# Queries stored raw and rotated one head ahead, one root for all heads, the late modulations moved into the merge stage

## The chip, the cores and the metric

The kernel runs on one core of a Trainium2 chip. The metric is the time of one execution in microseconds on the device. Of the core's engines this text speaks of TensorE (PE in the profile: matrix products, with its weight loads as PEld), VectorE (DVE), ScalarE (ACT), GpSimd (POOL) and SyncE (SP, which issues most of the DMAs). Each engine has a queue of its own, in which its instructions stand in a fixed order.

## What is computed

One layer of a diffusion backbone: 1024 latent tokens of width 1024, a context of 256 tokens, everything in float32. Cut to what matters here:

```python
mod_lat = silu(c) @ w_mod + b_mod                 # 9 pieces ml[0..8]; mc[..] for the context
x  = x  + 0.5*ml[2] * swiglu(modulate(rms_norm(x,  norm1_g), ml[0], ml[1]), ffn1_w_in, ffn1_w_out)
cx = cx + 0.5*mc[2] * swiglu(modulate(rms_norm(cx, norm1_g), mc[0], mc[1]), ffn1_w_in, ffn1_w_out)
hx, hc = modulate(rms_norm(x, norm2_g), ml[3], ml[4]), modulate(rms_norm(cx, norm2_g), mc[3], mc[4])
bg, cg, vc, q, k, v, gates = split(hx @ w_in)     # keys and values of the context from hc
y_conv = bg * short_conv(cg * vc, conv_w)
q, k = rotate(rms_norm(q, q_norm_g)), rotate(rms_norm(k, k_norm_g))   # 8 query heads, 2 key heads of 128
o = attend(q, concat(k_ctx, k), concat(v_ctx, v))
g_conv, g_attn = split(sigmoid(gates))
x  = x + ml[5] * ((g_conv * (y_conv @ w_branch_conv) + g_attn * (o @ w_branch_attn)) @ w_out)
x  = x + 0.5*ml[8] * swiglu(modulate(rms_norm(x, norm3_g), ml[6], ml[7]), ffn2_w_in, ffn2_w_out)
return rms_norm(x, final_g)
```

## The kernel before

**Products.** Every float32 operand of a product is split into a high part (rounded by ACT, a CAST in the profile) and a low part (the difference, taken by DVE or POOL), and each product of 128 columns is three matmuls: high by high, high by low, low by high. The large products against `w_in` and `ffn_w_in` are made by a Winograd scheme: POOL and DVE form sums of weight tiles (`s`), DVE their low parts (`wl`), and DVE and ACT combine the results out of PSUM (tiles `u`, `v`, `b`, `c`).

**Stages.** In the profile the first FFN takes about 140 to 980 us, the products of `w_in` (the "mix" stage, a list of 26 jobs `mix_jobs`) 980 to 1531, attention 1531 to 1945, the merge with `w_branch_attn` 1945 to 2040, `w_out` to 2140, and the second FFN and the end the rest.

**Order.** The body of the kernel is written as Python generators that are stepped against each other (`run(steps, n)` takes n steps). A scheduler then replays the recorded program with a timeline of its own and sets each engine's order by it, within the pools: `apool` (tag "A", 38 buffers of 128x1024), `tpool` (11 of 128x512), `wpool` for weights (3 raw, 4 high and 4 low), and PSUM banks (5 `ps`, 2 `pt`, 1 `po`). All instructions are recorded by one helper (L88), so a row of the profile is told by its tile names. Buffer names carry running numbers, which differ between the two programs.

**Mix (L1360 and on).** A job "uv" multiplies two results to `u`; from the third on it also runs 13 steps of the late modulations (`late_steps`, L1056 and L1368): modulation pieces 6, 7 and 8, each as two halves, each half 8 steps of a 256 KB load `rawm` and one DVE operation on `macc`, then `acch`, `accl` and a small product whose row goes to DRAM and back as `mcol`. What is left of them runs in the second FFN (L1766). Jobs "conv" write `yd`, jobs "gates" write sigmoids to `gad`. Job "k" and the four jobs "q" go through `turned` (L1267): for each result tile the 32-row pieces are swapped by DMA within SBUF into `sw`; ACT squares into `sq`; 8 small matmuls with `ones` sum the squares into PSUM; DVE multiplies by the cosine table, POOL multiplies `sw` by the sine table, DVE adds. For queries the root is left for later: `query_norm` takes the sums, finds the reciprocal root by ten small DVE operations per head and chunk (`rsqrt_cols`, tiles `rs_y` and `rs_t`) and keeps it in `rq`; the rotated query goes to DRAM (`qd`). For keys the root is broadcast and multiplied in before the store to `kd`. `turning_tables` makes the two tables by 16 PE transposes and 4 DVE operations, once for the keys and, at the first "q" job, once for the queries.

**Attention (L1407 on).** `k_ctx`, `keys_values(0)`, `v_ctx`, two weight tiles `wc` and the eight tiles `y` of the first chunk are loaded and split. 16 units (8 heads by 2 chunks of 512 queries) follow. `Unit.begin` loads 256 KB of `qd`, ACT rounds it and POOL takes the low part (`qs`). `scores` multiplies with keys, DVE takes maxima (`m`, `nm`) and multiplies by the query's root, ACT takes the exponential with that root as its scale. Products of the conv branch (`y`, `wc`) fill the gaps.

**Merge.** `merge(j, ch)` is called for 8 column blocks by 2 chunks; 14 of the 16 calls stand in the loop after attention. Each is 24 matmuls, then DVE on `ga` and `z`.

## Time and profile before

| | us |
|---|---|
| median of 3 runs | 2788.38 (2787.86 to 2788.5) |
| the profiled execution | 2791.95 |
| its span | 2790.2 |
| mean granted PE clock | 0.977 |

Engines' busy times, the stretches and the single stalls on which the argument rests stand in the prediction. In a window row the columns are: the stretch, its length, then for PE, PEld, DVE, ACT and POOL the busy time and (x) the instructions, the granted PE clock, the busy share of the DMA engines, and GB/s. A timeline row is: start, length, engine, line, operation, out<-in, shape, count, and in brackets the idle time before it with what ended it. In the list of tiles, three numbers with slashes are the shortest, the median and the longest in ns. Of the DMA issues the columns are the queue, the count, the size of each and the median us from issue to landing.

### The profile page before, as it was taken

Reading aid. Unit: us, or ns where it says so; the run is one execution under the profiler, and the core shown is the slowest. Engines: PE = TensorE matmul, PEld = TensorE weight load, DVE = VectorE, ACT = ScalarE, POOL = GpSimd, SP = SyncE. Lnnn points to the kernel's source line nnn. Section 1 sums busy time; section 2 is a strip of 40 time slices with the busy share of each in tenths; the row PEclk is TensorE's granted clock in tenths of the full one; section 3 lists DMA queues with packets and bytes.
Section 4 is the critical chain, followed back from the end, with each engine's and each line's share of the span. In section 5 each row is a group of like instructions: output and inputs, shape, how many; then the busy total and the mean of one; then the engine's idle time right before and its main releaser. Section 6 shows DMA issues by size and latency. Waiting matters only on the chain. (4 is left out here: it accounts for less than half of the span.)

```text
span 2790.2 us, 36733 instructions
## 1 busy us (share of the span) xinstructions
PE 2680.9 (96%) x13135; PEld 2230.4 (80%) x13135; DVE 2052.5 (74%) x3508; ACT 1149.8 (41%) x2144; POOL 567.9 (20%) x383
## 2 busy tenths in 40 slices
PE   7898999999999989999989999999999999999998
PEld 4687888888878867887868778887888788888888
DVE  5887688877877888768778576677547886567885
ACT  4524333333444632322324566666225333334443
POOL 2240112222010033233332111100000443221200
PEclk8899999999999999999999999999999999999999
DMA  8265433444984345334345421101443552327831
GB/s 302 91 202 156 140 122 99 129 132 156 321 201 109 113 146 179 121 106 129 110 125 158 146 91 59 46 23 35 147 136 106 181 167 91 101 78 268 196 87 61
DMA packets 374176, 374.27 MB, mean 134 GB/s; under 512 B 29782, under 2 KB 257256, under 8 KB 373992
## 3 DMA queue, kind: packets, MB, share of 16 engines
q1 hardware_dynamic: 364968, 354.61, 39.4%
q0 software_dynamic: 9024, 17.30, 3.8%
q8 instruction: 103, 1.69, 0.2%
q14 instruction: 81, 0.66, 0.1%
HBM read 295.77 MB, written 70.78 MB: 131 GB/s over the span
## 5 line engine op out<-in xcount | busy, mean ns | idle before, releaser
L88 PE MATMUL ps<-r,wl 128*128 128x512 f32 x5784 | 1365.7, 395 | 41.9 <-DVE wl L88 15.7
L88 PEld LDWEIGHTS ps<-r,wl 128*128 128x128 f32 x5784 | 1091.8, 190 | 281.3 <-DVE wl L88 21.9
L88 ACT CAST wl<-s 128x512 fp32r<-128x512 f32 x280 | 172.7, 619 | 373.6 <-PE ps L88 291.8
L88 ACT CAST wl<-raw 128x512 fp32r<-128x512 f32 x298 | 184.1, 619 | 300.2 <-PE ps L88 178.9
L88 POOL TENSOR_TENSOR s<-raw 128x512 f32<-128x512 f32 x70 | 104.2, 1489 | 936.5 <-DMA raw<-in_ffn_w_in_dram 531.3
L88 DVE TENSOR_TENSOR wl<-raw,wl 128x512 fp32r<-128x512 f32 x296 | 213.8, 723 | 94.1 <-ACT wl L88 93.0
L88 DVE TENSOR_TENSOR wl<-s,wl 128x512 fp32r<-128x512 f32 x280 | 240.1, 858 | 11.0 <-ACT wl L88 9.4
L88 POOL TENSOR_TENSOR s<-raw,s 128x512 f32<-128x512 f32 x70 | 112.3, 1604 | 447.2 <-DVE wl L88 436.3
L88 DVE SCALAR_TENSOR_TENSOR macc<-rawm,silu_c,macc 128x512 f32<-128x512 f32 x168 | 144.8, 881 | 9.4 <-DMA rawm<-in_w_mod_dram 8.6
L88 DVE TENSOR_REDUCE m<-ps 128x1 f32<-128x512 f32 (+1 forms) x192 | 111.2, 594 | 54.7 <-PE ps L88 53.5
L88 DVE TENSOR_TENSOR u<-u,ps 128x512 f32<-128x512 f32 x186 | 126.3, 680 | 32.4 <-PE ps L88 31.7
L88 DVE TENSOR_TENSOR pts<-pt,pts 128x512 fp32r<-128x512 f32 x160 | 108.5, 684 | 32.7 <-ACT pts L88 31.6
L88 PE MATMUL po<-pts,vl 128*128 128x512 f32 x384 | 130.0, 422 | 1.7 <-ACT pts L88 1.5
L88 PE MATMUL ps<-rh,wl 128*128 128x512 f32 x360 | 123.5, 393 | 2.8 <-ACT rh L88 2.8
L88 ACT CAST rh<-hid 128x512 fp32r<-128x512 f32 x132 | 81.2, 620 | 102.9 <-PE ps L88 85.9
L88 ACT CAST pts<-pt 128x512 fp32r<-128x512 f32 x160 | 91.5, 592 | 74.3 <-PE pt L88 72.4
L88 POOL TENSOR_TENSOR s<-raw,raw 128x512 f32<-128x512 f32 x70 | 107.9, 1541 | 23.0 <-DMA kcd<-kx 8.7
L88 PE MATMUL ps<-kl,qs 128*128 128x512 f32 x384 | 107.4, 399 | 1.2 <-ACT pc L88 1.0
L88 POOL TENSOR_TENSOR s<-s,raw 128x512 f32<-128x512 f32 x70 | 104.4, 1492 | 20.4 <-issue 5.8
L88 DVE TENSOR_TENSOR rl<-hid,rh 128x512 fp32r<-128x512 f32 x132 | 89.7, 684 | 21.8 <-PE ps L88 13.0
L88 PE MATMUL ps<-rh,wh 128*128 128x512 f32 x300 | 102.4, 389 | 0.0
L88 ACT ACTIVATE pl<-ps,nm,rq 128x512 f32<-128x512 f32 x128 | 98.5, 780 | 0.0
(308 smaller groups left out, 4635.7 us busy)
## 6 DMA issues: line engine op xcount, KB each, us to landing
raw<-in_ffn_w_in_dram SPq DMA_DIRECT2D x117, 512.0 KB, 4.6
raw<-in_ffn_w_out_dram SPq DMA_DIRECT2D x72, 512.0 KB, 5.3
rawm<-in_w_mod_dram SPq DMA_DIRECT2D x128, 256.0 KB, 3.6
raw<-in_w_in_dram SPq DMA_DIRECT2D x61, 512.0 KB, 4.6
hid<-hd SPq DMA_DIRECT2D x40, 512.0 KB, 9.3
ws<-in_ffn_w_out_dram POOLq DMA_DIRECT2D x30, 512.0 KB, 6.3
hd<-c SPq DMA_DIRECT2D x38, 256.0 KB, 2.0
hd<-u SPq DMA_DIRECT2D x38, 256.0 KB, 3.9
```

What stands on the lines that cost most here:

```text
L88: inst = getattr(self.engine, name)(*args, **kw)
```

## The change

- **Late modulations.** The uv jobs no longer run them. The merge loop takes one late step at every step of a merge (8 a merge, 112 of the 114 steps in the 14 merges), the loop in the second FFN takes what is left. So 32 operations on `macc` (with 8 MB of loads) leave the mix stage and 16 leave the second FFN; all 48 now stand at the end of attention and in the merge.
- **Queries.** A "q" job squares, sums by the 16 small matmuls, adds the sums to `rq` by one DVE operation for two heads, and stores the raw result. The DMAs into `sw`, 32 DVE operations of 128x512 and 16 POOL operations of 128x512 leave the mix stage, and so do the roots; one `rsqrt_cols` over 64 columns is put behind the last sums.
- **Rotation.** `turning_tables(0)` and `prepare_query(0)` stand at the end of the mix stage, behind the last product. `prepare_query` loads a whole head (512 KB) and, in four pieces, its swapped rows (512 KB), and POOL multiplies both and adds: three operations of 128x1024 a head, 24 in all. Head 1 is prepared at the start of attention, head n/2+1 in the even units n. `begin` splits a slice of the prepared head and loads nothing.
- **Keys.** Both multiplications and the addition are on POOL (12 operations of 128x512 there instead of 4, 8 fewer on DVE), and the roots are taken per head, so four times ten small operations on four columns in place of two times ten on eight.

```diff
@@ -224,10 +224,9 @@
             matmul(ps, wh, xl, start=False, stop=False)
             matmul(ps, wl, xh, start=False, stop=(i == last))
 
-    def rsqrt_cols(a, n):
-
-        y = small("rs_y", n)
-        t = small("rs_t", n)
+    def rsqrt_cols(a, n, yt=None):
+
+        y, t = yt or (small("rs_y", n), small("rs_t", n))
         dve.tensor_scalar(
             out=y[:].bitcast(I32), in0=a.bitcast(I32), scalar1=-0.5, scalar2=1597463007.0,
             op0=ALU.mult, op1=ALU.add,
@@ -1264,7 +1263,27 @@
                        pinned=True)
         return pss
 
-    def turned(dst, h0, ab, ch, tabs, norm):
+    def rsqrt_sums(pss):
+        a = small("rs_a", 4)
+        dve.tensor_scalar(out=a[:], in0=pss, scalar1=HD * EPS, scalar2=None, op0=ALU.add)
+        return rsqrt_cols(a[:], 4)
+
+    def queries(h0, ab, ch):
+
+        sq = atile("sq", (P, 2, 512))
+        for h, t in enumerate(ab):
+            act.activation(out=sq[:, h], in_=t, func=AF.Square)
+            sp.dma_start(out=qd[h0 + h, :, ch[1] : ch[1] + 512], in_=t)
+        yield
+        c0 = ch[1] // P
+        dve.tensor_scalar(
+            out=rq[:].rearrange("p (h t) -> p h t", t=KD)[:, h0 : h0 + 2, c0 : c0 + 4],
+            in0=square_sums([sq[:, h] for h in range(2)]).rearrange("p (h t) -> p h t", t=4),
+            scalar1=HD * EPS, scalar2=None, op0=ALU.add,
+        )
+        yield
+
+    def keys(ab, ch, tabs):
 
         o = ch[1]
         sw, sq = atile("sw", (P, 2, 512)), atile("sq", (P, 2, 512))
@@ -1273,36 +1292,31 @@
                 sp.dma_start(out=sw[a : a + 32, h], in_=t[b : b + 32])
             act.activation(out=sq[:, h], in_=t, func=AF.Square)
         yield
-        scale = norm(square_sums([sq[:, h] for h in range(2)]))
+        pss = square_sums([sq[:, h] for h in range(2)])
         for h, t in enumerate(ab):
-            dve.tensor_mul(out=t, in0=t, in1=tabs[0][:, o : o + 512])
+            pool.tensor_mul(out=t, in0=t, in1=tabs[0][:, o : o + 512])
             pool.tensor_mul(out=sw[:, h], in0=sw[:, h], in1=tabs[1][:, o : o + 512])
-            dve.tensor_add(out=t, in0=t, in1=sw[:, h])
-            if scale is None:
-                sp.dma_start(out=dst[h0 + h, :, o : o + 512], in_=t)
-        yield
-        if scale is not None:
-            for h, t in enumerate(ab):
-                pr = bcast(scale[:, 4 * h : 4 * h + 4], 512)
-                dve.tensor_mul(out=t, in0=t, in1=pr)
-                sp.dma_start(out=dst[h0 + h, :, o : o + 512], in_=t)
-        yield
-
-    def query_norm(h0, ch):
-        def norm(pss):
-            c0 = h0 * KD + ch[1] // P
-            for h in range(2):
-                a = small("ssq", 4)
-                dve.tensor_scalar(out=a[:], in0=pss[:, 4 * h : 4 * h + 4], scalar1=HD * EPS, scalar2=None, op0=ALU.add)
-                y = rsqrt_cols(a[:], 4)
-                dve.tensor_copy(out=rq[:, c0 + h * KD : c0 + h * KD + 4], in_=y[:])
-
-        return norm
-
-    def key_norm(pss):
-        a = small("ssk", 8)
-        dve.tensor_scalar(out=a[:], in0=pss, scalar1=HD * EPS, scalar2=None, op0=ALU.add)
-        return rsqrt_cols(a[:], 8)
+            pool.tensor_add(out=t, in0=t, in1=sw[:, h])
+        scale = [rsqrt_sums(pss[:, 4 * h : 4 * h + 4]) for h in range(2)]
+        yield
+        for h, t in enumerate(ab):
+            pr = bcast(scale[h], 512)
+            dve.tensor_mul(out=t, in0=t, in1=pr)
+            sp.dma_start(out=kd[h, :, o : o + 512], in_=t)
+        yield
+
+    q_turned = {}
+
+    def prepare_query(hd, tabs):
+
+        q, sw = atile("q"), atile("qsw")
+        load(q[:], qd[hd])
+        for a, b in swapped:
+            load(sw[a : a + 32], qd[hd, b : b + 32])
+        pool.tensor_mul(out=q[:], in0=q[:], in1=tabs[0][:])
+        pool.tensor_mul(out=sw[:], in0=sw[:], in1=tabs[1][:])
+        pool.tensor_add(out=q[:], in0=q[:], in1=sw[:])
+        q_turned[hd] = q
 
     def context_keys(pc):
         k, sq = ttile("kx"), ttile("ksq")
@@ -1311,9 +1325,7 @@
         later.append(context_keys_normed(k, sq))
 
     def context_keys_normed(k, sq):
-        a = small("ssk", 4)
-        dve.tensor_scalar(out=a[:], in0=square_sums([sq]), scalar1=HD * EPS, scalar2=None, op0=ALU.add)
-        y = rsqrt_cols(a[:], 4)
+        y = rsqrt_sums(square_sums([sq]))
         yield
         pr = bcast(y, 512)
         dve.tensor_scalar(
@@ -1364,8 +1376,6 @@
             for ch, cg, vc in pairs_of:
                 dve.tensor_mul(out=u[:, ch[1] : ch[1] + 512], in0=cg, in1=vc)
             run(normc2, 3)
-            if i > 1:
-                run(late_steps, 13)
         elif what == "conv":
             u = us.pop(i)
             for ch, bg, gc in pairs_of:
@@ -1389,17 +1399,17 @@
         elif what == "v":
             later.append(latent_values(pairs_of))
         else:
-            if i == 0:
-                tabs = turning_tables(int(what == "k"))
+            if what == "k":
+                tabs = turning_tables(1)
             for ch, a, b in pairs_of:
-                if what == "k":
-                    work = turned(kd, 0, (a, b), ch, tabs, key_norm)
-                else:
-                    work = turned(qd, 2 * i, (a, b), ch, tabs, query_norm(2 * i, ch))
+                work = keys((a, b), ch, tabs) if what == "k" else queries(2 * i, (a, b), ch)
                 next(work)
                 later.append(work)
+    tabs = turning_tables(0)
+    prepare_query(0, tabs)
     while later:
         run_later()
+    rstd_q = rsqrt_cols(rq[:], NQ * KD, [const.tile([P, NQ * KD], F32, name=f"rsq_{i}") for i in range(2)])
 
 
     k_lat, v_lat = {}, {}
@@ -1461,10 +1471,9 @@
             self.hd, self.ch, self.g = hd, ch, hd // (NQ // NKV)
 
         def begin(self):
-            o, q = self.ch[1], ttile("q")
-            load(q, qd[self.hd, :, o : o + 512])
+            o = self.ch[1]
             self.qs = [ttile("qs", dt=F32R) for _ in range(2)]
-            split(q, *self.qs, pool)
+            split(q_turned[self.hd][:, o : o + 512], *self.qs, pool)
             self.pc = atile("pc", (P, 4, CT))
             self.pl = []
             self.rsum = small("rsum", 4)
@@ -1492,10 +1501,10 @@
                 parts.append((pl[:, j * 512 : (j + 1) * 512], ps))
             dve.tensor_reduce(out=nm[:], in_=m3[:], axis=AX.X, op=ALU.max, negate=True)
             c = self.hd * KD + self.ch[1] // P + qt
-            dve.tensor_mul(out=nm[:], in0=nm[:], in1=rq[:, c : c + 1])
+            dve.tensor_mul(out=nm[:], in0=nm[:], in1=rstd_q[:, c : c + 1])
             for j, (dst, ps) in enumerate(parts):
                 act.activation(
-                    out=dst, in_=ps, func=AF.Exp, bias=nm[:], scale=rq[:, c : c + 1], accum_out=rs[:, j : j + 1]
+                    out=dst, in_=ps, func=AF.Exp, bias=nm[:], scale=rstd_q[:, c : c + 1], accum_out=rs[:, j : j + 1]
                 )
             dve.reduce_sum(out=self.rsum[:, qt : qt + 1], in_=rs[:], axis=AX.X)
 
@@ -1579,6 +1588,7 @@
     units = [Unit(hd, ch) for hd in range(NQ) for ch in (C0, C1)]
     u = units[0]
     u.begin()
+    prepare_query(1, tabs)
     run(conv_out(C0, 0))
     conv_weights(2)
     u.scores(0)
@@ -1612,6 +1622,8 @@
         u.begin()
         if n_unit == 4:
             keys_values(1)
+        if n_unit % 2 == 0 and n_unit < 14:
+            prepare_query(n_unit // 2 + 1, tabs)
         for n in (3, 2, 3, 2):
             u.scores(len(u.pl))
             for _ in range(n):
@@ -1636,7 +1648,9 @@
     for j in range(KD):
         for ch in (C0, C1):
             if (j, ch) not in ((0, C0), (1, C0)):
-                run(merge(j, ch))
+                step = merge(j, ch)
+                for _ in step:
+                    run(late_steps, 1)
     xs = Latents("x2")
     gain3 = norm_gain("gain3", 6, "g3")
     fast = Winograd(xs, gain3["l"], modl, 6, column_pairs(ffn2_w_in[0], ffn_offsets), ahead=AH3)
```

How the scheduler places this shows at three places. The first is SP's queue around the last gates of the mix stage (their stores are `gad`). Of before, up to the last of them (`kd`, `vd` hold keys and values, `yd` the conv inputs):

```order
L88 DMA kc_13471<-kcd 128x512
L88 DMA kl_13475<-kd 128x512
L88 DMA kl_13479<-kd 128x512
...
L88 DMA y_13507<-yd 128x512
...
L88 DMA y_13535<-yd 128x512
L88 DMA gad<-c_13348 128x512
L88 DMA raw_13576<-in_w_branch_conv_dram 128x8x128
L88 DMA q_13539<-qd 128x512
L88 DMA gad<-b_13384 128x512
...
L88 DMA gad<-u_13347 128x512
```

And of the change:

```order
L88 DMA gad<-c_12823 128x512
L88 DMA rope_12948<-in_rope_dram 128x512
...
L88 DMA gad<-b_12859 128x512
L88 DMA gad<-v_12858 128x512
L88 DMA gad<-u_12822 128x512
L88 DMA q_12980<-qd 128x1024
L88 DMA qsw_12981<-qd 32x1024 x4
L88 DMA kc_13002<-kcd 128x512
L88 DMA kl_13006<-kd 128x512
L88 DMA kl_13010<-kd 128x512
...
L88 DMA y_13038<-yd 128x512
```

All loads of attention stood ahead of the store of the last gate; now they all stand behind it, with the head's 1 MB first.

The second is PE's queue from the last product of the mix stage on. Of before:

```order
L88 MATMUL ps_13449<-r_1541_8839,wl_13403 128x512 x3
L88 MATMUL ps_13547<-y_13507,wc_13496 128x512 x2
L88 MATMUL ps_13547<-y_13507,wc_13497 128x512
L88 MATMUL ps_13547<-y_13511,wc_13496 128x512 x2
L88 MATMUL ps_13547<-y_13511,wc_13497 128x512
```

And of the change:

```order
L88 MATMUL ps_12924<-r_1541_8839,wl_12878 128x512 x3
L88 MATMUL pt_12949<-ident,rope_12948 128x128 x4
L88 MATMUL pt_12957<-ident,rope_12956 128x128 x4
L88 MATMUL pt_12965<-ident,rope_12964 128x128 x4
L88 MATMUL pt_12973<-ident,rope_12972 128x128 x4
L88 MATMUL ps_13086<-y_13038,wc_13027 128x512
L88 MATMUL ps_13121<-kc_13002,qs_13070 128x256 x2
L88 MATMUL ps_13130<-kl_13006,qs_13070 128x512 x2
L88 MATMUL ps_13135<-kl_13010,qs_13070 128x512 x2
```

Before, 24 matmuls of the conv branch (eight tiles `y`) came ahead of the first scores; now the transposes of the tables come, one conv matmul, and then the scores with the first head's `qs`.

The third is POOL's queue in the change, at the keys (`rope` are the tables, `s` the weight sums of the products that run meanwhile):

```order
L88 TENSOR_TENSOR c_10251<-c_10251,rope_10440 128x512
L88 TENSOR_TENSOR sw_10474<-sw_10474,rope_10441 128x512
L88 TENSOR_TENSOR c_10251<-c_10251,sw_10474 128x512
L88 TENSOR_TENSOR b_10311<-b_10311,rope_10440 128x512
L88 TENSOR_TENSOR sw_10474<-sw_10474,rope_10441 128x512
L88 TENSOR_TENSOR u_10250<-u_10250,rope_10440 128x512
L88 TENSOR_TENSOR sw_10486<-sw_10486,rope_10441 128x512
L88 TENSOR_TENSOR b_10311<-b_10311,sw_10474 128x512
L88 TENSOR_TENSOR s_1878_10720<-raw_10718 128x512
```

Before, only the products with the sine table stood here, and DVE had the others.

## The prediction

> **What bounds the kernel now.** First the head of the page and its chain of waits:
>
> ```profile
> span 2790.2 us, 36733 instructions
> PE 2680.9 (96%) x13135; PEld 2230.4 (80%) x13135; DVE 2052.5 (74%) x3508; ACT 1149.8 (41%) x2144; POOL 567.9 (20%) x383
> PE 40%; DVE 3%; DMA 1%; ACT 1%; issue 1%; POOL 0%; SPq 0%; DVEq 0%; ACTq 0%; POOLq 0%
> ```
>
> PE is busy for 96% of the span, and the chain is PE with short visits to others. Work taken from DVE or POOL is worth something only where PE waits, so I read windows of 20 us:
>
> ```profile
> 1060.00:1080.00 20.00, 20.00 (x90) 16.55 (x89) 13.23 (x20) 6.56 (x11) 10.53 (x7) 1.00 0.60 190
> 1100.00:1120.00 20.00, 17.00 (x64) 13.59 (x65) 15.71 (x26) 6.29 (x12) 8.09 (x6) 0.83 0.41 132
> 1300.00:1320.00 20.00, 15.76 (x67) 12.04 (x65) 20.00 (x55) 2.49 (x4) 6.47 (x4) 0.99 0.61 184
> 1460.00:1480.00 20.00, 15.44 (x73) 13.15 (x74) 17.74 (x31) 4.52 (x8) 8.94 (x6) 0.75 0.28 81
> ```
>
> A full window holds 90 large matmuls at clock 1.00, 0.222 us each. The windows that fall short lie where the late modulations or the query rotation run. The timeline names the stalls, on PE (first four rows) and on DVE:
>
> ```profile
> 1103.00 3.35 PE L88 MATMUL ps<-r,wl 128*128 128x512 f32 x7 [4.47 <-ACT wl L88]
> 1321.54 3.78 PE L88 MATMUL ps<-r,wl 128*128 128x512 f32 x8 [5.52 <-ACT u L88]
> 1434.25 5.30 PE L88 MATMUL ps<-r,wl 128*128 128x512 f32 x22 [3.22 <-DVE wl L88]
> 1464.56 5.73 PE L88 MATMUL ps<-r,wl 128*128 128x512 f32 x13 [8.50 <-DVE wl L88]
> 1092.07 6.60 DVE L88 SCALAR_TENSOR_TENSOR macc<-rawm,silu_c,macc 128x512 f32<-128x512 f32 x7 [0.90 <-DMA rawm<-in_w_mod_dram]
> 1428.91 0.69 DVE L88 TENSOR_TENSOR c<-c,rope 128x512 f32<-128x512 f32 x1 [4.90 <-DMA sw<-c]
> 1456.31 0.69 DVE L88 TENSOR_TENSOR c<-c,rope 128x512 f32<-128x512 f32 x1 [3.99 <-DMA sw<-c]
> 1456.92 1.29 DVE L88 SCALAR_TENSOR_TENSOR rs_y<-rs_t,rs_y 128x4 f32<-128x4 f32 x2
> 1462.48 0.23 DVE L88 SCALAR_TENSOR_TENSOR rs_t<-rs_y 128x4 f32<-128x4 f32 x2
> 1458.09 1.26 POOL L88 TENSOR_TENSOR s<-raw 128x512 f32<-128x512 f32 x1
> ```
>
> Seven `macc` hold DVE for 6.60 us and PE waits 4.47; twice DVE waits for the swapped rows, and behind it the small root operations take 1.29 us for what takes 0.23 when POOL is idle.
>
> **Mix stage: -29.** The idle times add up to 4.47 + 5.52 + 3.22 + 8.50 = 21.7 us. The first matmuls after them are slow: 7, 8, 22 and 13 took 18.16 us where 50 x 0.222 = 11.1 would do, so 7.1 more. All of it comes from operations that leave the stage: 28.8, taken as -29. The bounds are the idle time alone, -22, and -33 if smaller stalls of the same windows go too. What remains of a query job (squares, the small matmuls, one addition) is off the path.
>
> What would pay in the second FFN is nothing: PE fills this window with the `macc` in it.
>
> ```profile
> 2200.00:2320.00 120.00, 120.00 (x531) 99.13 (x530) 96.87 (x130) 37.60 (x63) 50.37 (x35) 1.00 0.53 163
> ```
>
> **The start of attention: +17.** Call the end of the last product T.
>
> ```profile
> 1530.69 0.61 PE L88 MATMUL ps<-y,wc 128*128 128x512 f32 x2
> 1532.28 5.28 PE L88 MATMUL ps<-y,wc 128*128 128x512 f32 x22 [0.97 <-DVE wc L88]
> 1519.74 4.33 SPq L88 DMA_DIRECT2D y<-yd  x6
> y<-yd SPq DMA_DIRECT2D x8, 256.0 KB, 6.0
> gcd<-b SPq DMA_DIRECT2D x1, 256.0 KB, 2.0
> 1534.85 0.64 ACT L88 ACTIVATE u<-u 128x512 f32<-128x512 f32 x1 [0.67 <-DVE u L88]
> 1532.07 0.62 ACT L88 CAST qs<-q 128x512 fp32r<-128x512 f32 x1 [0.32 <-DMA q<-qd]
> L88 POOL TENSOR_TENSOR wc<-raw,wc 128x1024 fp32r<-128x1024 f32 x9 | 21.6, 2395 | 111.5 <-ACT wc L88 111.5
> 1185.55 1.03 PE L88 MATMUL pt<-ident,rope 128*128 128x128 f32 x8
> 1528.61 1.89 DVE L88 TENSOR_TENSOR y<-y 128x512 fp32r<-128x512 f32 x3
> 1430.79 1.74 DVE L88 TENSOR_TENSOR c<-c,sw 128x512 f32<-128x512 f32 x1 [0.59 <-POOL sw L88]
> ```
>
> At T = 1530.69 PE went straight on, since the `y` loads had been issued by 1524. In the change they stand behind the last gate's store. That store waits for a DVE sum (0.67) and a sigmoid (0.64) after the last product: about T+1.5. SP then issues the head and its four swapped pieces at 4.33/6 = 0.72 each, to T+5.1; with 2.0 us of landing the head is there at T+7. POOL's three operations of 128x1024 take 3 x 2.395 = 7.2, ACT's rounding 0.62: the first scores can run at T+14.9. The first `y` is the thirteenth issue (five, then seven loads, then itself), at T+10, ready near T+13; only one matmul runs on it before the scores. PE has 16 transposes, 2 us, until then: 12.9 idle. To that come 2.8 us of slow matmuls (13 after the 8.50 stall took 5.73 for 2.9), and about 3 for DVE, which now takes 14 low parts here (0.63 alone, by the row of three; 1.74 beside POOL). What the start costs today, 2, goes: 12.9 + 2.8 + 3 - 2 = 17. Bounds: 9, if issues take 0.38 as single ones do and the low parts keep pace, and 26, if POOL's operations stretch by a third and half the low parts take 1.74.
>
> **Keys: +5.** POOL now has a train of 12 rotations with 4 `s` between, and the DVE rows ahead of the next `wl` hold some 38 small operations.
>
> ```profile
> 1200.00:1220.00 20.00, 18.70 (x90) 15.19 (x89) 12.32 (x45) 1.28 (x3) 4.60 (x4) 0.91 0.13 46
> 1190.72 1.82 POOL L88 TENSOR_TENSOR sw<-sw,rope 128x512 f32<-128x512 f32 x1 [12.41 <-DMA sw<-c]
> 1200.80 1.80 POOL L88 TENSOR_TENSOR sw<-sw,rope 128x512 f32<-128x512 f32 x1
> 1206.40 0.31 DVE L88 SCALAR_TENSOR_TENSOR rs_y<-rs_t,rs_y 128x8 f32<-128x8 f32 x3
> 1204.85 11.07 PE L88 MATMUL ps<-r,wl 128*128 128x512 f32 x48
> ```
>
> Today POOL is done at 1202.6 and the small operations run at 0.1 each. The train of 16 by 1.3 to 1.75 from 1190.7 lasts to 1212 or 1218, and about eight of the small operations then take 1.29: some 9 us later for `wl`, of which the 48 matmuls in hand (11.07 us) cover about half. +5, between 0 and 12.
>
> **POOL within attention: +5.**
>
> ```profile
> 1540.00:1940.00 400.00, 384.92 (x2064) 314.79 (x2063) 265.22 (x607) 261.48 (x603) 40.88 (x24) 0.99 0.20 63
> L88 DVE TENSOR_TENSOR nm<-nm,rq x64: 127/150/1146, 1541.2 to 1923.8; 128x1 f32<-128x1 f32 x64
> ```
>
> The 21 further operations add 50 us to POOL's 41. `nm` takes 150 ns, at worst 1146, when it meets POOL; an eighth more of its 64, each waiting half of 2.4, is 8 x 1.2 = 10 us on the way to the exponentials, half of it hidden: +5, from 0 to 12.
>
> In the Trainium skill, "SBUF — State Buffer", section "Who interferes with whom", a DVE operation with two SBUF inputs and a POOL operation lock each other out for a whole instruction. By that rule a 128x1024 rotation would hold a low part for up to 2.4 us, where the row above has 1.74 beside 128x512; it makes the third rival, and the 1.29 against 0.23 bears it out.
>
> **The moved modulations: +3 and +5.**
>
> ```profile
> 1900.00:1940.00 40.00, 34.66 (x194) 26.51 (x191) 28.88 (x64) 28.97 (x64) 0.00 (x0) 1.00 0.08 27
> 1960.00:2040.00 80.00, 80.00 (x355) 66.24 (x354) 41.27 (x56) 19.61 (x26) 0.00 (x0) 1.00 0.50 160
> 300.00:600.00 300.00, 298.80 (x1717) 262.08 (x1716) 234.58 (x359) 101.44 (x184) 69.80 (x43) 1.00 0.38 120
> L88 DVE SCALAR_TENSOR_TENSOR macc<-rawm,silu_c,macc x168: 732/742/1880, 30.7 to 2316.8; 128x512 f32<-128x512 f32 x168
> ```
>
> The first half falls into the last units, where PE already waits 5.3 of 40 us: 8 x 0.74 on a DVE with 11 us to spare; +3, from 0 to 5. The other 40 come into the merge, where PE is full and DVE has 41.3 of 80. They add 40 x 0.74 and five `accl`, 33 us: DVE at 74 of 80. The first FFN shows PE full with DVE at 78%, no stretch shows 93%. Loads grow from 160 GB/s by 40 x 0.262 MB in 80 us, 131, to 291. PE has the slack of several banks, and the operations are spread one by one, unlike the seven in a row above: +5, from 0 to 12.
>
> **The sum.** -29 + 17 + 5 + 5 + 3 + 5 = +6. Profiled, 2791.95 + 6 = 2798; the median of the runs lies 3.6 below the profiled execution, so 2794.4.
>
> **The rivals.**
> 1. *Faster: the gap at T is short and nothing else bites.* One mechanism: the head's chain at its quickest, with the first conv matmuls and scores back to back after it. The gap costs 9, the keys 0, attention 2, the late units and the merge 2: -29 + 13 = -16, 2772. For it: a merge stage with half its DVE free, no PE wait on POOL in the chain. Against it: the queue rows, which put 1 MB and a POOL chain of 7.2 us ahead of anything PE can do. It decides if PE's gap at T stays under about 11 us.
> 2. *Slower: the merge becomes bound by DVE.* At 93% any wait of a `macc` on its load stands ahead of the `ga` sums and `wl`; five halves each with one wait of 3 us give 15 in place of 5: 2804. Against it, the loads are issued ahead of need.
> 3. *Slower: POOL and DVE lock each other out by the instruction.* Fourteen low parts behind rotations of 2.4 us each, and the same for `nm`: 26 at the start and 12 in attention, 16 more than the sum: 2810.
> 4. The change not doing what it says is excluded by the queue rows for the moves; only where the scheduler's guess is wrong can a queue stand still.
>
> **Chances.** The forecast 0.41, the first rival 0.33, the second 0.13, the third 0.13. A measurement of this kernel tells 0.2% (5.6 us) from no change. The forecast's own spread, 2784 to 2802, is about 0.17 within that and 0.24 slower, with the first rival wholly faster: faster 0.33, same 0.17, slower 0.50. The range: the low bounds together reach 2764, the high ones 2833; they will not meet, and 2768 to 2814 leaves out 2 in 10.
>
> **What would show it.** Right: the four PE stalls at 1103, 1321, 1434 and 1464 are gone and those windows read 20.00; the span to T is some 24 us shorter; then one PE wait of 11 to 16 us on ACT's `qs` or `y`; POOL in 1540 to 1940 near 90 us. Wrong in a term: a stall by the keys of 0 or over 12, merge windows with PE under 19. Wrong as a whole: attention's first matmul within 8 us of T, or the mix stage still losing 10 us or more.

## The result, and the profile after

| | before | changed |
|---|---|---|
| median of 4 runs, us | 2788.44 | 2813.22 (2807.68 to 2818.24) |
| ratio | 1 | 1.0088, interval 1.0065 to 1.011 |
| span of the profiled execution, us | 2790.2 | 2805.9 |

The change makes the kernel slower, by 24.8 us in the medians, where the forecast was +6; 2813.2 lies just inside the range's upper end of 2814. The profiled execution of the changed kernel was the fastest of its four, so at the end of the experiments each kernel was profiled once more. The four spans divide by events that both programs have: T is the end of the last mix product, the next marks are the first `rinv` transpose, the first matmul on `oh` (merge) and the first and last on `mh` (`w_out`).

| us | before, two profiles | changed, two profiles | mean difference | forecast |
|---|---|---|---|---|
| to T | 1530.7, 1527.7 | 1496.8, 1500.0 | -30.8 | -29 and keys +5 |
| T to the first `rinv` | 73.5, 71.8 | 92.3, 92.1 | +19.5 | +17 |
| attention from there | 337.7, 337.1 | 351.8, 351.5 | +14.2 | +5 and +3 |
| merge | 93.3, 93.2 | 95.2, 95.3 | +2.0 | +5 |
| `w_out` | 88.3, 88.3 | 104.7, 107.3 | +17.7 | 0 |
| the rest | 666.7, 670.9 | 665.1, 672.1 | -0.2 | 0 |
| span | 2790.2, 2789.0 | 2805.9, 2818.3 | +22.5 | +6 |

The stages after T repeat within 3 us, so the differences of 14 to 30 stand clear of them. The rest moves by 4 to 7 between two profiles of the same kernel.

The head of the page, to set beside that of before:

```profile
span 2805.9 us, 36392 instructions
PE 2685.9 (96%) x13135; PEld 2231.4 (80%) x13135; DVE 2017.3 (72%) x3316; ACT 1155.8 (41%) x2144; POOL 610.8 (22%) x399
```

DVE has 35 us less to do and POOL 43 more, and the busy share of PE is still 96%. As before, only the windows tell where. First the three of the mix stage, at the times of before, then the keys, attention, the merge and two of `w_out`:

```profile
1100.00:1120.00 20.00, 20.00 (x90) 16.56 (x89) 18.27 (x27) 5.62 (x10) 11.52 (x7) 1.00 0.34 105
1300.00:1320.00 20.00, 20.00 (x90) 16.57 (x89) 14.93 (x23) 6.75 (x11) 5.24 (x4) 1.00 0.36 119
1460.00:1480.00 20.00, 20.00 (x90) 16.53 (x90) 13.98 (x22) 6.12 (x10) 6.03 (x4) 1.00 0.25 79
1200.00:1220.00 20.00, 17.08 (x81) 13.69 (x82) 13.88 (x31) 4.17 (x7) 4.26 (x3) 1.00 0.34 106
1540.00:1940.00 400.00, 377.12 (x2016) 306.51 (x2015) 275.28 (x604) 255.20 (x589) 81.33 (x40) 0.99 0.23 69
1960.00:2040.00 80.00, 80.00 (x353) 65.23 (x352) 51.69 (x76) 20.82 (x29) 0.00 (x0) 1.00 0.59 182
2040.00:2060.00 20.00, 12.75 (x49) 9.57 (x47) 10.38 (x18) 2.42 (x4) 0.00 (x0) 0.91 0.56 181
2060.00:2080.00 20.00, 15.89 (x59) 12.56 (x60) 15.86 (x22) 4.62 (x6) 0.00 (x0) 0.83 0.99 346
```

The mix windows are full now, and so are all others from 1080 to 1480 but the two by the keys (19.43 at 1180, 17.08 at 1200). The merge is full too, with DVE at 51.7 of 80 and not the 74 that was worked out. The hole is behind it: 108 matmuls in the 40 us from 2040, where 180 fit; the missing 72 at 0.222 us are 16.0 us, all but 0.4 of what `w_out` loses in this profile. In the profile of before the same 40 us are full:

```profile
2040.00:2060.00 20.00, 20.00 (x90) 16.57 (x89) 7.90 (x8) 4.21 (x4) 0.00 (x0) 1.00 0.42 124
2060.00:2080.00 20.00, 20.00 (x90) 16.57 (x89) 6.87 (x8) 4.22 (x4) 0.00 (x0) 1.00 0.37 106
```

The start of attention came as it was worked out. The timeline of the changed kernel there, PE, then SP, then POOL, then DVE:

```profile
1496.77 1.03 PE L88 MATMUL pt<-ident,rope 128*128 128x128 f32 x8
1499.51 1.32 PE L88 MATMUL pt<-ident,rope 128*128 128x128 f32 x8 [1.70 <-DVE rope L88]
1511.03 0.79 PE L88 MATMUL ps<-y,wc 128*128 128x512 f32 x1 [10.21 <-ACT y L88]
1511.62 0.77 PE L88 MATMUL ps<-kc,qs 128*128 128x256 f32 x2
1498.34 0.32 SPq L88 DMA_DIRECT2D gad<-u  x1
1498.75 0.38 SPq L88 DMA_DIRECT2D q<-qd  x1
1499.23 1.80 SPq L88 DMA_DIRECT2D qsw<-qd  x4
1503.49 2.34 POOL L88 TENSOR_TENSOR q<-q,rope 128x1024 f32<-128x1024 f32 x1 [23.33 <-DMA q<-qd]
1508.21 2.68 POOL L88 TENSOR_TENSOR q<-q,qsw 128x1024 f32<-128x1024 f32 x1
1514.86 12.51 DVE L88 TENSOR_TENSOR y<-y 128x512 fp32r<-128x512 f32 x8
```

T is 1496.77. The last gate's store goes out at T+1.57, the head has landed at T+6.7, POOL's three operations end at T+14.1, and the first scores run at T+14.85. PE is idle for 10.21 + 1.70 us, and DVE's eight low parts then take 12.51 where 8 x 0.63 = 5.0 is their own length. Beside them POOL rotates head 1.

### The profile page after: what moved, and what is told of

Read it like the earlier page. It is cut to its first block, busy times and chain, and to the rows that moved or that the text cites. A ratio compares the mean times of both kernels' runs of the same rounds, so it can differ in the third digit from the quotient of the medians.

```text
span 2805.9 us, 36392 instructions
## 1 busy us (share of the span) xinstructions
PE 2685.9 (96%) x13135; PEld 2231.4 (80%) x13135; DVE 2017.3 (72%) x3316; ACT 1155.8 (41%) x2144; POOL 610.8 (22%) x399
## 4 chain that ended last, share of the span: by engine, by line
PE 82%; DVE 8%; DMA 4%; issue 3%; ACT 2%; POOL 1%; SPq 1%; DVEq 0%; ACTq 0%; POOLq 0%
PE ps L88 67%; PE po L88 8%; PE pt L88 7%; DVE wl L88 1%; DMA raw<-in_ffn_w_out_dram 1%; DVE nt L88 1%; DVE r L88 1%; DMA raw<-in_ffn_w_in_dram 1%; SPq L88 1%; DVE macc L88 1%; DVE m L88 1%; DVE y L88 0%; DVE pts L88 0%; DMA qsw<-qd 0%; DVE rs_t L88 0%
## 5 line engine op out<-in xcount | busy, mean ns | idle before, releaser
L88 POOL TENSOR_TENSOR s<-raw 128x512 f32<-128x512 f32 x70 | 107.3, 1533 | 933.1 <-DVE r L88 366.1
L88 DVE TENSOR_REDUCE m<-ps 128x1 f32<-128x512 f32 (+1 forms) x192 | 111.7, 595 | 51.7 <-PE ps L88 47.8
L88 ACT CAST pts<-pt 128x512 fp32r<-128x512 f32 x160 | 92.0, 593 | 93.3 <-PE pt L88 90.5
L88 PE MATMUL ps<-y,wc 128*128 128x512 f32 x384 | 100.8, 405 | 14.4 <-ACT y L88 10.2
```

What stands on the lines that cost most here:

```text
L88: inst = getattr(self.engine, name)(*args, **kw)
```

## The experiments

All of them in one table, by the stages above, with each one's median against the median of before on the same chip. Of each there is one profile. T differs by up to 6 us between profiles of the same mix stage (1496.8 to 1503.0 for the change and experiments 6, 7 and 10), the rest by 7, the other stages by less than 3.

| kernel | T | start | attention | merge | `w_out` | rest | ratio (interval) |
|---|---|---|---|---|---|---|---|
| before, first | 1530.7 | 73.5 | 337.7 | 93.3 | 88.3 | 666.7 | |
| the change, first | 1496.8 | 92.3 | 351.8 | 95.2 | 104.7 | 665.1 | 1.0088 (1.0065 to 1.011) |
| 1 late modulations alone | 1503.2 | 70.5 | 339.8 | 95.3 | 109.1 | 662.7 | 0.998 (0.997 to 0.999) |
| 2 queries and keys alone | 1515.8 | 92.3 | 346.1 | 93.2 | 88.3 | 674.7 | 1.005 (1.0032 to 1.0068) |
| 3 the change, old keys | 1493.5 | 93.7 | 352.0 | 95.3 | 103.8 | 670.4 | 1.0063 (1.0046 to 1.008) |
| 4 first head prepared earlier | 1508.5 | 72.3 | 354.4 | 95.2 | 103.3 | 670.3 | 1.0039 (1.0025 to 1.0053) |
| 5 late alone, 78 steps in the merge | 1497.1 | 69.5 | 340.3 | 94.3 | 91.0 | 667.7 | 0.9918 (0.9899 to 0.9937) |
| 6 root as scalar operand | 1496.9 | 93.8 | 355.8 | 95.2 | 103.6 | 670.0 | 1.0093 (1.0073 to 1.0112) |
| 7 heads prepared in odd units | 1503.0 | 93.7 | 349.4 | 95.3 | 103.0 | 664.1 | 1.007 (1.0051 to 1.009) |
| 8 edits 4 to 7 together | 1503.4 | 72.1 | 344.6 | 95.6 | 91.4 | 674.2 | 0.9994 (0.9981 to 1.0007) |
| 9 as 5, four buffers held | 1502.9 | 69.2 | 338.9 | 94.4 | 93.0 | 673.6 | 0.9937 (0.9915 to 0.9958) |
| 10 heads 1 to 7 not rotated | 1499.5 | 88.7 | 338.7 | 94.4 | 107.0 | 665.3 | 1.0029 (1.0016 to 1.0042) |

### 1 to 4: the parts of the change

Experiment 1 is the kernel before with only the late modulations moved:

```diff
             run(normc2, 3)
-            if i > 1:
-                run(late_steps, 13)
...
-                run(merge(j, ch))
+                step = merge(j, ch)
+                for _ in step:
+                    run(late_steps, 1)
```

> The kernel before with one part of the change alone: the late modulations leave the uv jobs and are taken one step at a time in the merge loop. Theory (four separate terms, as the two traces show them): the mix stage is 8 to 14 us shorter (the seven macc in a row are gone, the rotation stays), the end of attention costs 3 to 4, and PE stands 11 us and more at the head of w_out waiting for DVE's ga, in all 16 to 18 there: 2794 to 2802. Rival (the stall in w_out comes from attention's other delays, not from the moved steps): no PE wait on ga, 2776 to 2782.

Experiment 2 is the changed kernel with those lines turned back, so with the new queries and keys alone.

> The changed kernel with the late modulations put back into the uv jobs and the second FFN; queries and keys as changed. Theory: the wait on ga and the slow end of attention go, about 20 us, and the macc bursts come back, 8 to 14: 2798 to 2806, with a gap on y at the start of attention of 10 us as in the changed kernel and w_out full. Rival: the w_out stall stays, 2815 to 2825.

Experiment 1 took 2784.0 us, less than was expected of it, since the mix stage became 26 us shorter and not 8 to 14. The late modulations alone bring T 26 us forward, nearly the whole gain of the mix stage, and already lose 20.8 in `w_out`; the queries and keys alone bring 13.4 and lose 19.6 at the start and 8.7 in attention. The gains don't add up: 39.4 apart, 30.8 together. Why shows when the four stalls of before are looked for one by one. A stall must be sought at the same work and not at the same time: in experiment 1, T comes 27.5 us earlier, so the stall that stood at 1464, 66 us ahead of T, would stand near 1437. It is there. Two windows of experiment 1, then PE and DVE at that place (before had 8.50 on PE and 3.99 on DVE):

```profile
1100.00:1120.00 20.00, 20.00 (x90) 16.53 (x90) 17.18 (x27) 5.88 (x10) 10.99 (x7) 1.00 0.35 108
1420.00:1440.00 20.00, 14.56 (x54) 11.47 (x54) 17.08 (x63) 3.18 (x6) 5.51 (x5) 0.84 0.35 106
1437.54 10.51 PE L88 MATMUL ps<-r,wl 128*128 128x512 f32 x34 [5.44 <-DVE wl L88]
1429.53 1.82 DVE L88 TENSOR_TENSOR c<-c,rope 128x512 f32<-128x512 f32 x1 [2.92 <-DMA sw<-c]
```

With the rotation left in the mix stage, DVE still waits there for the swapped rows and PE for DVE; the other three stalls are gone. In experiment 2, where the late steps are back and the rotation is gone, it is the other way round: the first stall stands and that of the swapped rows is gone (its place is now near 1450).

```profile
1105.56 16.61 PE L88 MATMUL ps<-r,wl 128*128 128x512 f32 x60 [3.51 <-ACT wl L88]
1100.00:1120.00 20.00, 16.49 (x62) 12.98 (x61) 15.04 (x23) 5.08 (x9) 7.67 (x5) 0.83 0.41 132
1440.00:1460.00 20.00, 20.00 (x93) 16.70 (x91) 9.48 (x14) 6.73 (x11) 3.11 (x3) 0.94 0.26 81
```

So the stall of the seven `macc` goes with the late modulations alone, and the last one in full only with the rotation. The two between them, 5.52 and 3.22 us, are gone in both experiments: they take both loads, and their gain is counted twice when the two parts are added.

Experiment 3 is the change with the keys rotated on DVE as before (POOL has the sine product alone, one root for both heads).

```diff
-            pool.tensor_mul(out=t, in0=t, in1=tabs[0][:, o : o + 512])
+            dve.tensor_mul(out=t, in0=t, in1=tabs[0][:, o : o + 512])
...
-            pool.tensor_add(out=t, in0=t, in1=sw[:, h])
-        scale = [rsqrt_sums(pss[:, 4 * h : 4 * h + 4]) for h in range(2)]
+            dve.tensor_add(out=t, in0=t, in1=sw[:, h])
```

> The changed kernel with the keys rotated and rooted as before (DVE multiplies and adds, two roots of eight columns). Theory: the keys' part of the change costs or gives next to nothing, 2808 to 2818, windows by the keys (1180 to 1240) within 2 us of the changed kernel's. Rival (the 5 us of the prediction are real and covered by a larger gain elsewhere in the mix stage): 5 us shorter by the keys, 2803 to 2808.

T is 3.3 us ahead of the earliest of the profiles with the new keys, which differ by more among themselves, and the ratios' intervals overlap, so the times tell nothing. The waits of PE between 1160 and 1260 do: they add up to 3.4 to 4.2 us in the five profiles that share the change's mix stage (the change twice, experiments 6, 7 and 10) and to 0.9 here, with none on `u` any more. The new keys cost about 3 us.

Experiment 4 prepares the first head, tables included, ahead of the last "conv" job, while PE still has products:

```diff
     for what, i, _, _ in mix_jobs:
+        if what == "conv" and i == 7:
+            tabs = turning_tables(0)
+            prepare_query(0, tabs)
...
-    tabs = turning_tables(0)
-    prepare_query(0, tabs)
     while later:
```

> The changed kernel with one thing moved: the query tables and the preparation of head 0 stand ahead of the last conv job of the mix stage instead of behind its last product, so the head's load and POOL's three operations and the loads of attention can go ahead of the last gates. Theory (the start of attention is a chain of load, POOL and rounding behind the last gate): the gap on y and the waits on DVE's low parts shrink to a few us, 2793 to 2800. Rival (it is DMA bandwidth or the buffers: the same loads press into the last jobs of the mix stage and PE waits there instead): 2805 to 2815.

The start falls from 92 to 72.3, what it was before, so the gap at T comes of the preparation and of the loads that stand behind it. But T is later, 1508.5 here and 1503.4 in experiment 8 with the same edit, where the five profiles without it have 1496.8 to 1503.0: in the means 6.7 us, a third of the gain, are given back. PE now waits for `wl` in the last jobs, three times by 1.2 to 1.5 us here. The time, 2800.9, lies between the two that were expected.

### 5: fewer late steps in the merge

Experiment 5 takes up the loss in `w_out`. It is experiment 1 with the first 78 late steps in the merge and the other 36 left to the second FFN:

```diff
+    early_late = (next(late_steps) for _ in range(78))
     for j in range(KD):
...
                 for _ in step:
-                    run(late_steps, 1)
+                    run(early_late, 1)
```

> The kernel before with only the late modulations moved, as in the run of that part alone, but the merge loop takes the first 78 steps and leaves the other 36 to the second FFN, as many as stood there before. Theory (w_out waits because the last merges' DVE sums ga stand behind the last macc, their loads and the DVE addition that waits for mcol; without late steps in the last four merges the tail is short): w_out takes 88 to 92 us as in the kernel before, and the time is 2763 to 2770. Rival (any late steps in the merge hold up ga or the loads of w_out): w_out stays above 100 us and the time at 2780 to 2786.

The loss is nearly gone (91.0 us for 88.3), and the whole kernel is faster than both: 2767.3 us, 0.9918 of before. The first row is of the changed kernel, the second of experiment 5, the numbers after the count being the shortest, median and longest in ns, then the first and the last start:

```profile
L88 PE MATMUL ps<-mh,wh x128: 387/389/796, 2036.1 to 2140.3; 128*128 128x512 f32 x128
```

```profile
L88 PE MATMUL ps<-mh,wh x128: 387/389/496, 2001.2 to 2091.8; 128*128 128x512 f32 x128
```

The operations that write or read `macc`, `accl` and `acch` among them, counted by stage (length, then DVE's time and count, then ACT's), first of the changed kernel:

```profile
1941.00:2036.00 95.00, 19.24 (x27) 1.87 (x3) 1.00 0.56 172
2036.00:2141.00 105.00, 12.83 (x18) 1.24 (x2) 0.95 0.54 168
```

And of experiment 5:

```profile
1907.00:2001.00 94.00, 19.28 (x27) 1.87 (x3) 1.00 0.56 174
2001.00:2092.00 91.00, 1.23 (x2) 0.00 (x0) 1.00 0.50 153
```

On DVE the merge has 27 of them in both, 24 additions to `macc` and three `accl`, and PE is full there in both. The difference is in `w_out`: 18 in the change (16 and two), 2 in experiment 5. The other 14 additions are back in the second FFN, where the kernel before has 14 too; by its trace 34 of the 48 that moved stand in its mix stage, where the section on the change gives 32 and 16.

### 6 and 7: how POOL costs attention time

Experiment 6 tests the prediction's own reason, that `nm` waits for POOL. The root goes in as the scalar of a tensor-scalar operation, which has one tensor input:

```diff
-            dve.tensor_mul(out=nm[:], in0=nm[:], in1=rstd_q[:, c : c + 1])
+            dve.tensor_scalar(
+                out=nm[:], in0=nm[:], scalar1=rstd_q[:, c : c + 1], scalar2=None, op0=ALU.mult
+            )
```

> The changed kernel, where the negated maximum nm is multiplied by the query's root as a scalar operand of a one-input operation instead of as a second tensor. Theory (two-input DVE operations wait for whole POOL operations; the 24 rotations in attention hold up nm and so the exponentials): nm falls from 265 ns in the mean to 150 to 170, the waits of PE on ACT pc (6.8 us) fall by half, attention from the first rinv to the last product 3 to 6 us shorter, 2806 to 2811. Rival (the scalar operand waits just the same, or nm is off the path): 2811 to 2818, nm above 240 ns.

The list of tiles shows `nm` in the change first, then in experiment 6:

```profile
L88 DVE TENSOR_TENSOR nm<-nm,rsq x64: 129/156/1786, 1529.1 to 1924.1; 128x1 f32<-128x1 f32 x64
```

```profile
L88 DVE TENSOR_SCALAR nm<-nm,rsq x64: 199/210/217, 1529.4 to 1928.0; 128x1 f32<-128x1 f32 x64
```

The long cases are gone, and attention gains nothing: 355.8 us for 351.7. The form itself takes 54 ns more at the median, and the 64 together 13.4 us for 16.7, so little more than 3 was to be gained here. But the traces of the two kernels say the same: the 64 took 11.1 us before, only 5.6 less than in the change, and PE's waits that end with `nm` in this stage fell from 3.6 to 1.5 us. So waiting of `nm` was not what cost the time.

Experiment 7 moves the preparation of heads 2 to 7 from the even units to the odd ones:

```diff
-        if n_unit % 2 == 0 and n_unit < 14:
+        if n_unit % 2 == 1 and 1 < n_unit < 14:
```

> The changed kernel with heads 2 to 7 prepared one unit earlier or later (odd units), so that head 3's rotation does not run while DVE makes the low parts of the second chunk's y. Theory (PE's longest wait in attention, 5.07 us at 1638, is three low parts of 1.7 to 2.2 us that each wait for a POOL rotation): that wait is gone, 2807 to 2813. Rival (the rotations meet some other DVE work there, and the sum stays): within 2 us of the changed kernel, with a wait of 4 us or more elsewhere in 1600 to 1700.

The longest wait of PE on `pts` falls from 5.07 to 1.1 us, but attention only by 2.3. PE's waits on `pc` grow there from 6.8 to 8.1 us, so the place of the preparation in part only moves the waits.

### 8: all mends together

> The changed kernel with all three, and the preparation of head 0 ahead of the last conv job: 78 late steps in the merge, nm by a scalar operand, heads prepared in odd units. Theory (separate terms that add): -16 to -20 at w_out, -12 at the start of attention as measured, -4 to -8 in attention: 2772 to 2784, under the kernel before. Rival (the terms share the same slack): 2786 to 2795.

The edits of 4, 6 and 7 and the 78 steps of 5 on the changed kernel end level with before, 0.9994. The start (72.1) and most of `w_out` (91.4) are mended, and attention has 7 us over before in place of 14. The single mends of the start and of `w_out`, though, were worth some 20 us (experiment 4) and 18 (experiment 5 beside 1) in their stages and do not lead below before in the medians (the profiled run, 5.9 us under the median, has a span 8 us shorter than before's two). The same 78 steps without the new queries (experiment 5) are 0.8% better than this.

### 9 and 10: buffers or POOL

What is left in attention could come from the rotations on POOL, or from the two buffers of 128x1024 that a prepared head takes from the 38 that attention shares. Experiment 9 takes four of those buffers away from experiment 5, from the start of attention until unit 13:

```diff
+    held = [atile("held") for _ in range(4)]
+    for t in held:
+        dve.memset(t[:, :1], 0.0)
...
+        if n_unit == 13:
+            for t in held:
+                dve.tensor_mul(out=t[:, :1], in0=t[:, :1], in1=units[12].rsum[:, :1])
```

> The kernel with 78 late steps in the merge and the old queries (2767), with four buffers of apool taken at the end of the mix stage and given back in unit 13, as the change holds two tables, a head and its swapped rows through attention. Theory (what attention lost beside the late macc, some 8 to 12 us, is the smaller pool: scores wait for a buffer of pl): attention from the first rinv to the first product of w_branch_attn by oh grows from 340 to 347 to 352. Rival (it is POOL's rotations): it stays at 338 to 343.

Attention takes 338.9 us, against 340.3 without the held buffers, where 347 to 352 was expected. The buffers are not the cause of attention's loss.

Experiment 10 is the change with the three POOL operations for the first head only; the loads and buffers of the other heads stay:

```diff
-        pool.tensor_mul(out=q[:], in0=q[:], in1=tabs[0][:])
...
+        if hd == 0:
+            pool.tensor_mul(out=q[:], in0=q[:], in1=tabs[0][:])
...
```

> The changed kernel without POOL's three operations for heads 1 to 7; their loads and buffers stay. It leaves the rotation of these heads out. Theory (buffers): attention by the same measure stays at 348 to 354. Rival (POOL's rotations hold DVE up): it falls from 352 to 340 to 345, and the whole to 2800 to 2806.

Attention falls by 13 us to 338.7, within 1.3 of before. The window of attention, which had 377.12 of PE in the change and 384.92 before:

```profile
1540.00:1940.00 400.00, 385.00 (x2073) 316.28 (x2072) 272.39 (x611) 259.88 (x596) 38.65 (x22) 0.99 0.24 72
```

The rotations alone cost it, not the 7 MB of loads beside them. PE's waits that end with `pts` fall from 11.1 to 6.8 us and those that end with `pc`, which ACT makes, from 6.8 to 1.0. Head 1 is rotated at the start; without that the eight low parts there take half as long, and the start is 3.5 us shorter (88.7):

```profile
1517.62 5.99 DVE L88 TENSOR_TENSOR y<-y 128x512 fp32r<-128x512 f32 x8
```

### 11 and 12: the two kernels once more

> The kernel before, for a second profile: how far the stages differ between profiles of one program. Theory (stage lengths hold within 3 us, so that the differences of 12 us and more between kernels are theirs): T at 1528 to 1534, T to the first rinv 72 to 75, attention 336 to 340, w_out 88. Rival: T differs by 6 us or more from 1530.7, so that what the mix stage gained is known only to that.

> The changed kernel for a second profile. Its first profile was of its fastest run (2807.7, the others to 2818.2). Theory (the rest of the 24.8 us is spread of single waits in the second FFN, as the 4 us wait on rl that the profiles of its variants show): T within 6 us of 1496.8, T to the first rinv 92 to 94, attention 349 to 356, w_out 103 to 109, and the part behind w_out 664 to 675. Rival: one of the four stages of the change differs by more than 6 us from the first profile.

The kernel before gave 2788.26, ratio 0.9993 (0.9979 to 1.0008); the change 2814.58, ratio 1.0071 (1.0054 to 1.0088). Their stages stand in the first table: the second profile of the change, of the slowest of its four executions, has the same losses in the same places, and the 22.5 us by which the mean spans differ fits the 24.8 and the 21.5 by which the medians do.

## Why the prediction was right in sign and short by some 17 us

**Mix stage, -29, and keys, +5.** Together -24 was forecast and -30.8 measured. The four stalls are gone and the windows are full, as was named. The keys took less than their +5: the window 1200 to 1220 shows 17.08, but PE's waits around the keys add up to 3.4 us and more where the old keys have 0.9 in the same place (experiment 3), so about 3, and the mix stage gave some 34 where its bound was 33. The split of the stalls holds for the first and the last, 4.47 us by `macc` and 8.50 by the swapped rows, of which 5.44 stand in experiment 1. For the two in the middle, of which one was put down to the swapped rows, it was too simple: they go when either load goes, so `macc` and the rotations together made DVE late there.

**The start, +17.** Measured +19.5, along the chain that was worked out, down to the first scores at T+14.85 where T+14.9 was forecast. The eight low parts of `y` took 7.5 us beyond their own length where about 3 was counted for all 14; the start is 3.5 us shorter in experiment 10, which takes most of that away. Which term holds the remaining 2.5 was not separated. The first rival was to be told by a gap under about 11 us, and the forecast by a wait of 11 to 16: the single wait is 10.21, the idle time with the 1.70 is 11.91, so the sign stood on the border. What felled the rival is its price, 9 us for the 19.5 measured. Experiment 4 shows that the chain is the cause, and that moving it ahead costs the mix stage about a third of the 20 us.

**POOL within attention, +5, and the last units, +3.** Measured +14.2. Experiment 1 gives 2.4 for the late operations in the last units. The other 12 are POOL's rotations by experiment 10, which takes 13 away; experiment 2, with the rotations and without the late modulations, has only 8.7, so the two cost more together. The step that failed is the one that named `nm` as what waits. Of the 21 further operations 18 run here, POOL being busy for 81.3 us where near 90 was named; head 1's three run at the start. What waits instead is seen about 1630 in the timeline of the change, DVE, POOL and PE in turn:

```profile
1629.16 0.68 DVE L88 TENSOR_TENSOR pts<-pt,pts 128x512 fp32r<-128x512 f32 x1
1630.36 1.69 DVE L88 TENSOR_TENSOR y<-y 128x512 fp32r<-128x512 f32 x1
1632.64 2.20 DVE L88 TENSOR_TENSOR y<-y 128x512 fp32r<-128x512 f32 x1
1635.49 2.10 DVE L88 TENSOR_TENSOR y<-y 128x512 fp32r<-128x512 f32 x1
1629.00 2.50 POOL L88 TENSOR_TENSOR q<-q,rope 128x1024 f32<-128x1024 f32 x1 [13.19 <-DMA q<-qd]
1631.81 2.48 POOL L88 TENSOR_TENSOR qsw<-qsw,rope 128x1024 f32<-128x1024 f32 x1 [0.31 <-DMA qsw<-qd]
1634.37 2.67 POOL L88 TENSOR_TENSOR q<-q,qsw 128x1024 f32<-128x1024 f32 x1
1638.40 0.97 PE L88 MATMUL pt<-ident,pl 128*128 128x128 f32 x4 [5.07 <-DVE pts L88]
```

POOL's operations end at 1631.50, 1634.29 and 1637.04; the three low parts of `y` end at 1632.05, 1634.84 and 1637.59, each 0.55 us later, which is about their own length. Each low part waited until POOL's running operation had ended. `pts`, which reads one of its inputs from PSUM, takes 0.68 as always in the middle of one. In the Trainium skill, "SBUF — State Buffer", section "Who interferes with whom", DVE operations with two SBUF inputs and POOL exclude each other for a whole instruction; the rows agree for DVE behind POOL, and experiment 6 as well, where `nm` with a single tensor input is never held; POOL behind DVE they don't show. In experiment 10 the eight low parts of this chunk take 0.68 to 0.69 each. They are one place among several: in experiment 7 they are free of POOL too, and attention gains only 2.3. This was the third rival's mechanism, put at 12 for attention: right there, but its `nm` was not what paid, and at the start, for which it had 26 (9 over the forecast), the lock is worth 3.5. By PE's waits, experiment 10 takes 4.3 us off `pts`, behind the low parts, and 5.8 off `pc`, so ACT is held as well; what holds ACT stays open, since its 6.9 us stand in experiment 6 too, where `nm` no longer waits.

**The merge, +5.** This term was mis-sized most: +2.0 in the merge and +17.7 in `w_out`, for which the sum had nothing. The prediction put 40 operations on `macc` and five `accl` into the merge; 27 of the 45 run there, 18 later. It also counted the operations and the bytes, and not the round trip that ends each half: ACT copies a row (`mrow`), SP scatters it by four DMAs to `mcol` (from SBUF to SBUF, not by way of DRAM), and DVE adds the bias (`modl`). The timeline of the change at the first holes of `w_out`, PE, then ACT, SP and DVE:

```profile
2045.21 0.80 PE L88 MATMUL ps<-mh,wh 128*128 128x512 f32 x1 [4.82 <-DVE ga L88]
2055.10 0.40 PE L88 MATMUL pt<-acch,ones_r 128*1 128x512 f32 x1
2063.77 0.79 PE L88 MATMUL ps<-mh,wh 128*128 128x512 f32 x1 [6.19 <-DVE ga L88]
2050.01 0.62 ACT L88 CAST acch<-macc 128x512 fp32r<-128x512 f32 x1 [3.37 <-DVE macc L88]
2056.23 0.57 ACT L88 COPY mrow<-pt 1x512 f32<-1x512 f32 x1 [4.99 <-PE pt L88]
2046.69 0.33 SPq L88 DMA_DIRECT2D rawm<-in_w_mod_dram  x1
2056.83 2.41 SPq L88 DMA_DIRECT2D mcol<-mrow  x4
2059.33 0.53 SPq L88 DMA_DIRECT2D ga<-gad  x1
2065.29 9.48 SPq L88 DMA_DIRECT2D x<-xd  x13
2060.79 0.16 DVE L88 TENSOR_TENSOR modl<-mcol,bcol 128x4 f32<-128x4 f32 x1 [8.44 <-DMA mcol<-mrow]
2063.03 0.69 DVE L88 TENSOR_TENSOR ga<-ga,ps 128x512 f32<-128x512 f32 x1 [2.07 <-DMA ga<-gad]
```

`acch` is ready at 2050.63, but its small matmul stands behind full ones in PE's queue until 2055.10. SP issues nothing from 2047.0 to 2056.83, because `mcol` is next in its queue and needs `mrow`; the load of `ga` stands behind it and goes out at 2059.33. DVE stands at `modl` for 8.44 us, then waits 2.07 for `ga`, and PE waits for DVE. PE, ACT, SP and DVE hold each other up through the order of their queues, none of them being busy. When SP is free, the held loads go out together (346 GB/s in that window). The second rival had this kind of wait, on a load ahead of `ga`, but in the merge and at 15; "the loads are issued ahead of need" was the argument against it, and it does not hold for a load that is queued behind a transfer of a result. Experiment 5 shows that the late steps make it: nearly without those in `w_out`, 91.0 us. It takes the loads, the operations and the round trip away together; that the round trip is what holds the queues is read from the timeline.

With the measured stages in place of the forecast ones, -30.8 + 19.5 + 14.2 + 2.0 + 17.7 - 0.2 = +22.4. The sign came out as forecast, though +6 left it nearly open, and with some luck: the mix stage gave about 7 us more than its term, which covered part of the 23 by which the others fell short. Short were the terms in which an engine waits for its place in a queue or for another engine's port, and not for time of its own.

## What to carry to other kernels

When work is moved into a stage because its engines have time to spare, follow the longest chain of the moved work through every queue, with what stands behind each step: here the cost was no operation's time but a row on its way through PE, ACT, SP and DVE. Try a moved load in smaller portions before giving it up: the late modulations alone were worth 0.2% at 112 steps in the merge loop and 0.8% at 78. Gains of parts that relieve the same engine do not add, and their losses may. Look for a stall of one program in another at the same work, counted from an event that both have, and not at the same time.

## What the runs showed of the hardware

A tensor-scalar operation on 128x1, with its second factor as the scalar operand in SBUF, took 199 to 217 ns in all 64 cases, in a stage in which POOL rotates six heads (experiment 6). The two-tensor form of the same product takes 156 at the median and up to 1786 (2215 in experiment 7), so the slower form is the steady one.
